# Weight-block sums from an accumulating DMA to VectorE, and the adaLN sums spread anew

## The chip, the cores and the metric

One core of one Trainium2 chip. The metric is the device time in microseconds of one execution; the time of a kernel is the median over its runs. The engines are named as in the profile: PE is TensorE (PEld its weight loads), DVE is VectorE, ACT is ScalarE, POOL is GpSimd, and SP is SyncE, which here issues nearly all DMAs.

## The reference

A two-layer trunk over 512 tokens of width 1024, in float32. Each layer is a token mixer and then a SwiGLU FFN, each between two RMSNorms, with shift, scale and gate from a conditioning vector `c` (adaLN):

```python
def ada_modulation(c, w, b):
    m = jax.nn.silu(c) @ w + b
    shift, scale, gate = jnp.split(m, 3, axis=-1)
...
for i in range(DEPTH):
    shift, scale, gate = ada_modulation(c, mix_ada_w[i], mix_ada_b[i])
    h = rms_norm(x, mix_pre_g[i]) * (1.0 + scale) + shift
    y = stick_breaking_mixer(...) if i % 2 == 0 else token_mixing_mixer(...)
    x = x + gate * rms_norm(y, mix_post_g[i])
    shift, scale, gate = ada_modulation(c, ffn_ada_w[i], ffn_ada_b[i])
    h = rms_norm(x, ffn_pre_g[i]) * (1.0 + scale) + shift
    y = (silu(h @ w_gate) * (h @ w_up)) @ w_down        # D_FF = 2816
    x = x + gate * rms_norm(y, ffn_post_g[i])
```

Layer 0 mixes with stick-breaking attention (16 heads), layer 1 with a gMLP (`u, v = split(gelu(h @ w_in))`, a layer norm and a position mixing of `v`, then `(u * v) @ w_out`).

## The kernel before

**Precision.** Every float32 product is made of three: `split` writes a high part (ACT copies into float32r) and a low part (DVE subtracts), and `mm3` issues high by high, high by low and low by high. So each 512 KB slab of weights costs one 128x1024 ACT copy (line 94) and one 128x1024 DVE subtraction (line 95) before PE can use it.

**Weights.** `stream` lists all slabs in the order of use. `wget` emits the splits some slabs ahead and `wload` the loads. Raw slabs live in `wraw` (2 buffers), split ones in `wpool` and `wpool2` (6 pairs in all).

**Stages in order.** Attention and its projection; a boundary (RMSNorms, adaLN, transposes of the new `h`); gate/up of FFN 0; its down projection; a boundary; the gMLP; a boundary; gate/up of FFN 1; its down projection. In each gate/up stage the first three of the 22 column groups are multiplied plainly (`unit`), the other 19 with a seven-product (Strassen-Winograd) scheme over two halves of tokens, of the inner dimension, and of gate against up (`seven`).

**A block of seven.** For each of the 19 blocks of a stage `block_loads` and `blocks` make the four sums of weight blocks that the scheme needs. `x` holds B11 and B22 and `y` holds B21 (`rawx`, `rawy`). `f13` holds T1 and T3: SP reads `wx` a second time into it, and a DMA on the POOL queue then adds the rest of `wy` with `accum_op=ALU.add` (line 152; in `wy` the block B12 lies twice for this). `f24` (T2, T4) is summed on DVE in two halves (lines 165 and 166). All are split. `seven` runs the products into three PSUM banks; between them ACT copies (lines 945, 949, 951) and DVE adds or subtracts (947, 953, 955), and PE goes on into the same banks. The last product (T4) can start when the subtraction of line 955 has read its bank; line 963 multiplies silu(gate) by up and ends the block.

**adaLN sums.** `ada_stt` (line 269) adds one 128x1024 slab of adaLN weights, scaled by a column of silu(c), to an accumulator on DVE: 8 sums for each of shift (B), scale (A) and gate (G) of a sub-layer. A `Bg` is a generator over such parts: first all sums, then for each part a reduction over partitions in two halves (split, two matmuls with ones into a bank `adaps`, an evacuation). `step(n)` advances it by n yields. The raw slabs `rawada` share the pool `raw2` (2 buffers) with `rawy`. Attention carries G0, A0 and B0. In the first gate/up stage `bg0` carries G1 and A1; in the first down stage `bg` carries B1 and G2 at two steps for each k until the cut `mid`, then `bg2` (A2, B2) at two steps for each k, with its rest in the gMLP; the second gate/up stage carries G3.

**The cut.** In the first down stage the sums over k of tile 0 lie in the two banks that `adaps` needs too. `mid` is the k at which they are copied out (`yp`), so that the reductions can run; it follows from the number of parts:

```python
mid = min(nk - J, -(-8 * len(bg.parts) // steps) + 1) if steps else None
```

With 2 parts and 2 steps `mid` is 9, with 3 parts it is 13; `nk - J` is 18.

**Order.** The order of each engine's instructions is made at compile time by a list scheduler from the program's order and the buffers; on the chip every engine and every DMA queue takes its instructions in that order. General slots (`slot`, pool `s4`) are 28 buffers of 4 KB per partition that hold nearly all activations.

Of the kernel before, what the change touches and what calls it, by code (L numbers as in the profile page):

```python
# [13 lines left out]
P = 128  # L14
# [12 lines left out]
def trunk(ctx: ExitStack, tc: tile.TileContext, A: dict, out: bass.AP):  # L27
# [110 lines left out]
    def block_loads(idx):  # L138

        fp = fwork["pool"]
        x = wraw.tile([P, KD, P], F32, tag="raw", name=nm("rawx"))
        y = fwork["raw"].tile([P, 4, P], F32, tag="raw2", name=nm("rawy"))
        f13 = fp.tile([P, KD, P], F32, tag="f13", name=nm("f13"))
        wx, wy = A["wx"][idx], A["wy"][idx]
        load(x[:], wx)
        load(f13[:], wx)  # L150
        load(y[:], wy[:, 0:4, :])
        nc.gpsimd.dma_start(out=f13[:], in_=wy[:, 4:12, :], accum_op=ALU.add)  # L152
        return x, y, f13

    def blocks(xr, yr, f13):

        fp = fwork["pool"]
        x = wtile(KD, P)
        split(x[0][:], x[1][:], xr[:])
        b21 = [fp.tile([P, 4, P], F32R, tag=f"b21{i}", name=nm("b21")) for i in range(2)]  # L160
        split(b21[0][:], b21[1][:], yr[:])
        t13 = wtile(KD, P)
        split(t13[0][:], t13[1][:], f13[:])
        f24 = fp.tile([P, KD, P], F32, tag="f24", bufs=1, name=nm("f24"))
        dve.tensor_tensor(f24[:, 0:4, :], f13[:, 0:4, :], xr[:, 4:8, :], ALU.add)
        dve.tensor_tensor(f24[:, 4:8, :], f24[:, 0:4, :], yr[:], ALU.add)
        t24 = wtile(KD, P)
        split(t24[0][:], t24[1][:], f24[:])

        def half(t, i):  # L170
            return lambda k: (t[0][:, 4 * i + k, :], t[1][:, 4 * i + k, :])

        return {
            "B11": half(x, 0), "B22": half(x, 1), "B21": half(b21, 0),
            "T1": half(t13, 0), "T3": half(t13, 1), "T2": half(t24, 0), "T4": half(t24, 1),
        }
# [98 lines left out]
    class Bg:  # L275
# [2 lines left out]

        def __init__(self, *parts):

            self.parts = [
                (n, int(s), int(s) + (n != "G"), {"G": 2, "A": 1, "B": 0}[n]) for n, s in parts
            ]
            self.gen = self.run()

        def run(self):
            for name, at, s, part in self.parts:
                acc = slot(F32, name, 1, D)[:, 0, :]  # L290
                ada[name, at] = acc
                nc.gpsimd.memset(acc, 0.0)
                load(acc[0:1, :], A["adab"][s, part])
                for k in range(KD):
                    raw = fwork["raw"].tile([P, D], F32, tag="raw2", name=nm("rawada"))
                    load(raw[:], A["ada"][s, part, k])
                    ada_stt(acc, raw[:], k)
                    yield
            for name, at, s, part in self.parts:
                acc = ada[name, at]  # L300
                if part:
                    row = A["pre_g"] if part == 1 else A["post_g"]
                    g = slot(F32, "g", 1, D)[:, 0, :]
                    load(g, row[s : s + 1, :].to_broadcast([P, D]))
                for b in range(2):
                    c = slice(b * 512, (b + 1) * 512)
                    h = adas.tile([P, 512], F32R, tag="acch", name=nm("acch"))
                    l = adas.tile([P, 512], F32R, tag="accl", name=nm("accl"))
                    split(h[:], l[:], acc[:, c])
                    yield  # L310
                    yield
                    ps = bank("adaps", "p")
                    mm(ps[:], ones_r, h[:], True, False, last_tp[0])
                    mm(ps[:], ones_r, l[:], False, True)
                    if part == 0:
                        act.activation(acc[:, c], ps[:], AF.Copy)
                    elif part == 1:
                        dve.scalar_tensor_tensor(acc[:, c], ps[:], 1.0, g[:, c], ALU.add, ALU.mult)
                    else:
                        dve.tensor_tensor(acc[:, c], ps[:], g[:, c], ALU.mult)  # L320
# [110 lines left out]
    def out_proj(s, nk, get_act, wkey, J, bg, hT, nxt=(), pre=None, S=None, steps=0, bg2=None):  # L431

        last = 0 if steps else 3
        mid = min(nk - J, -(-8 * len(bg.parts) // steps) + 1) if steps else None
        yp = None
        y = [[None, None] for _ in range(NT)]  # L440

        def step(k, tt, a, w, halves=(0, 1)):
            for hf in halves:
                if k == 0 or k == mid and tt == last:
                    y[tt][hf] = bank("y", "p" if tt == last else "b")
                mm3(
                    y[tt][hf][:],
                    a[0][:, tt * P : (tt + 1) * P], a[1][:, tt * P : (tt + 1) * P],
                    w[0][:, 0, hf * 512 : (hf + 1) * 512],
                    w[1][:, 0, hf * 512 : (hf + 1) * 512],  # L450
                    k == 0 or k == mid and tt == last, k == nk - 1 or k + 1 == mid and tt == last,
                )

        npre = 0
        if pre is not None:
            npre = len(pre["w"])
            for tt in pre["y"]:
                y[tt] = pre["y"][tt]
        for k in range(nk - J):
            a = get_act(k)  # L460
            w = pre["w"][k] if k < npre else wget(wkey(k))
            for tt in range(NT):
                if k >= npre or tt not in pre["y"]:
                    step(k, tt, a, w)
            bg.step(steps)
            if bg2 is not None and mid is not None and k >= mid:
                bg2.step(2)
            if k + 1 == mid:
                yp = slot(F32, "yp")
                for hf in range(2):  # L470
                    act.activation(yp[:, hf, :], y[last][hf][:], AF.Copy)
                bg.step(99)
        bg.step(99)
        tail = [
            (k, get_act(k), wget(wkey(k), J + 1 if k == nk - J else 0))
            for k in range(nk - J, nk)
        ]
        sqrt_table()
        xs = {tt: x_load(tt) for tt in range(2)}
        xin = xs.get  # L480
        for tt in range(NT):
            for hf in range(2):
                for k, a, w in tail:
                    step(k, tt, a, w, (hf,))
            if tt == last and yp is not None:
                for hf in range(2):
                    dve.tensor_tensor(yp[:, hf, :], y[tt][hf][:], yp[:, hf, :], ALU.add)
                y[tt] = [yp[:, hf, :] for hf in range(2)]
            if tt < 2:
                boundary(s, tt, y[tt], xin, hT, S, "p" if last == 0 else "b")  # L490
                xs[tt + 2] = x_load(tt + 2)
        evacs, late = [], []
        for n, tt in enumerate((2, 3)):
            if nxt:
                evacs.append(nxt[n]())
            late.append(boundary(s, tt, y[tt], xin, hT, S, "p" if tt == 3 else "b"))
        if nxt:
            evacs.append(nxt[2]())
            with tc.issue_after(last_sqrt[0].ins):
                for f in evacs:  # L500
                    f()
        if hT is not None:
            for f in late:
                f()
# [382 lines left out]
    class Ffn:  # L887
# [81 lines left out]
        def run(self, bg0, bg, bg2, steps, nhT, nxt, nS=None):  # L969
            for f in range(NH):  # L970
                self.unit(f, 256, 256)()
            for f in range(NH, KF):
                self.seven(f)()
                bg0.step(1 + (f % 3 == 0))
            bg0.step(99)
            out_proj(
                self.s, KF, lambda k: act_split(self.act[k // 2][:, k % 2, :]),
                lambda k: ("wdown", self.li, k), 4, bg, nhT, nxt, None, nS, steps, bg2,
            )
# [21 lines left out]
        return evac  # L1001

    uw = {}
    STEPS = 1

    def u_first(hT, ms):
        ev = []
# [5 lines left out]
    def gmlp(bg, hT, nhT, nS, nxt):  # L1013
# [114 lines left out]
    )  # L1128
    bg2 = Bg("A2", "B2")
    f0.run(  # L1130
        Bg("G1", "A1"), Bg("B1", "G2"), bg2, 2, hT2,
        [lambda a=a: u_first(hT2, range(a, min(a + 2, NU))) for a in range(0, NU, 2)],
    )
    gmlp(bg2, hT2, hT3, S3, f1.first())
    f1.run(Bg("G3"), bg2, None, 0, None, ())


def _layout(i):
# [7 lines left out]
    def blocks(a, b):  # L1146

        return (
            np.concatenate([a[:, :, :4], b[:, :, 4:]], 2),
            np.concatenate([a[:, :, 4:], b[:, :, :4], b[:, :, :4]], 2),  # L1150
        )

    def slabs(w):
# [77 lines left out]
```

## Time and profile before

| | us |
|---|---|
| median of 3 runs | 1222.86 (1219.6 to 1223.47) |
| the profiled execution | 1221.21 |
| its span, first to last instruction | 1219.5 |
| PE busy | 1176.3 |
| DVE busy | 846.6 |
| ACT busy | 621.3 |
| POOL busy | 51.4 |

The HBM moved 194.44 MB in and 8.39 MB out. The mean granted clock of PE was 0.998. In the profile a matmul's duration is longer than its share of PE, since matmuls overlap: those of 256 columns last 0.28 us and start 0.117 us apart, those of 512 columns last 0.395 us and start 0.232 us apart. So a block's length is read from the distance between starts, and what PE loses from its idle time before an instruction.

### The profile page before, as it was taken

The numbers are of one execution on the slowest core, as the hardware profiler recorded it, in microseconds if no ns is written. First come the engines' busy times: TensorE is split into PE (matmuls) and PEld (weight loads), VectorE is DVE, ScalarE is ACT, GpSimd is POOL, SyncE is SP. The second block draws the span as 40 slices with busy tenths as digits, with TensorE's granted clock in tenths as the row PEclk, the third lists the DMA queues.
The fourth block names the chain that finished last, engine by engine and source line by source line (L and its number), as shares of the span: only waits on it lengthen the run. The fifth ranks groups of instructions, "written<-read, shape, count | busy, mean of one in ns | idle before, by whom it ended". The sixth has DMA issues, their size and how long they took to land.

```text
span 1219.5 us, 18827 instructions
## 1 busy us (share of the span) xinstructions
PE 1176.3 (96%) x7408; PEld 1031.6 (85%) x7408; DVE 846.6 (69%) x1183; ACT 621.3 (51%) x1071; POOL 51.4 (4%) x68
## 2 busy tenths in 40 slices
PE   7898999999999999999999999999999999999997
PEld 4777778787899889998888898898998999998886
DVE  5878887766797787777787764567977777774223
ACT  6455767785564444556252453535644555573212
POOL 0100000000000010001000000000000001000000
PEclk9999999999999999999999999999999999999999
DMA  8666341121648868776888453314477777635311
GB/s 332 231 203 203 114 139 53 50 72 54 187 135 240 231 199 250 216 193 187 276 277 294 156 173 106 102 70 138 134 206 234 214 182 182 156 106 176 100 52 69
DMA packets 59580, 204.05 MB, mean 167 GB/s; under 512 B 6874, under 2 KB 7002, under 8 KB 59492
## 3 DMA queue, kind: packets, MB, share of 16 engines
q1 hardware_dynamic: 52292, 176.64, 43.2%
q0 software_dynamic: 7200, 26.22, 11.2%
q8 instruction: 58, 0.95, 0.3%
q14 instruction: 30, 0.25, 0.1%
HBM read 194.44 MB, written 8.39 MB: 166 GB/s over the span
## 4 chain that ended last, share of the span: by engine, by line
PE 66%; DVE 14%; DMA 11%; issue 4%; ACT 4%; DVEq 0%; SPq 0%; ACTq 0%
PE y L71 24%; PE r L71 19%; DMA rawada<-in_ada 7%; PE v L71 5%; PE pqk L71 4%; DVE wl L95 4%; PE u L71 3%; PE av L71 2%; PE z3h L71 2%; PE z0h L71 2%; DMA raw<-in_wgu 1%; PE gu L71 1%; ACT wh L94 1%; PE tp L79 1%; PE z2h L71 1%
## 5 line engine op out<-in xcount | busy, mean ns | idle before, releaser
L71 PE MATMUL y<-wh,as 128*128 128x512 f32 x832 | 263.5, 395 | 0.3 <-ACT gu L960 0.3
L94 ACT ACTIVATE wh<-raw 128x1024 fp32r<-128x1024 f32 x112 | 118.4, 1059 | 205.4 <-PE y L71 111.5
L95 DVE TENSOR_TENSOR wl<-raw,wh 128x1024 fp32r<-128x1024 f32 x112 | 136.6, 1221 | 123.4 <-ACT wh L94 123.3
L71 PEld LDWEIGHTS y<-wh,as 128*128 128x128 f32 x832 | 156.2, 188 | 37.0 <-ACT gu L960 0.7
L71 PE MATMUL r<-Sh,wh 128*128 128x256 f32 x608 | 171.7, 282 | 7.1 <-ACT e L951 4.1
L71 PE MATMUL r<-Sh,wl 128*128 128x256 f32 x608 | 170.2, 280 | 0.0
L71 PE MATMUL r<-Sl,wh 128*128 128x256 f32 x608 | 170.0, 280 | 0.0
L71 PE MATMUL y<-wl,as 128*128 128x512 f32 x416 | 164.3, 395 | 0.0
L94 ACT ACTIVATE wh<-f 128x1024 fp32r<-128x1024 f32 x76 | 80.7, 1061 | 92.0 <-PE r L71 82.6
L71 PEld LDWEIGHTS r<-Sh,wh 128*128 128x128 f32 x608 | 114.6, 189 | 10.2 <-ACT e L951 6.0
L71 PEld LDWEIGHTS r<-Sl,wh 128*128 128x128 f32 x608 | 114.5, 188 | 0.0
L71 PEld LDWEIGHTS r<-Sh,wl 128*128 128x128 f32 x608 | 114.4, 188 | 0.0
L95 DVE TENSOR_TENSOR wl<-f,wh 128x1024 fp32r<-128x1024 f32 x76 | 92.7, 1220 | 29.1 <-ACT wh L94 29.1
L71 PE MATMUL r<-hTh,wh 128*128 128x256 f32 x304 | 88.9, 294 | 8.3 <-DVE gu L955 8.0
L71 PEld LDWEIGHTS y<-wl,as 128*128 128x128 f32 x416 | 78.2, 188 | 18.1
L71 PE MATMUL r<-hTl,wh 128*128 128x256 f32 x304 | 84.9, 280 | 0.0
L71 PE MATMUL r<-hTh,wl 128*128 128x256 f32 x304 | 80.5, 281 | 0.0
L71 PEld LDWEIGHTS r<-hTh,wh 128*128 128x128 f32 x304 | 57.2, 188 | 15.1 <-DVE gu L955 12.3
L269 DVE SCALAR_TENSOR_TENSOR G<-rawada,sc,G 128x1024 f32<-128x1024 f32 x32 | 41.1, 1283 | 41.3 <-DMA rawada<-in_ada 39.2
L71 PE MATMUL r<-hTh,b 128*128 128x256 f32 x304 | 61.7, 286 | 0.0
L152 POOL DMA_DIRECT2D f<-in_wy x38 | 33.2, 881 | 645.6 <-ACT wh L94 262.6
L71 PEld LDWEIGHTS r<-hTl,wh 128*128 128x128 f32 x304 | 57.4, 189 | 0.2
(245 smaller groups left out, 2669.3 us busy)
## 6 DMA issues: line engine op xcount, KB each, us to landing
rawada<-in_ada SPq DMA_DIRECT2D x80, 512.0 KB, 4.3
raw<-in_wdown SPq DMA_DIRECT2D x44, 512.0 KB, 4.2
f<-in_wx SPq DMA_DIRECT2D x38, 512.0 KB, 4.9
f<-in_wy POOLq DMA_DIRECT2D x38, 512.0 KB, 5.9
rawx<-in_wx SPq DMA_DIRECT2D x38, 512.0 KB, 5.3
rawy<-in_wy SPq DMA_DIRECT2D x38, 256.0 KB, 2.9
raw<-in_wqk SPq DMA_DIRECT2D x16, 512.0 KB, 4.5
ada<-in_ada0p SPq DMA_DIRECT2D x12, 512.0 KB, 5.6
```

Source lines behind the costliest of these rows:

```text
L71: b = nc.tensor.matmul(o, l, r, start=start, stop=stop, skip_group_check=True)
L79: last_tp[0] = nc.tensor.transpose(o, i, ident)
L94: act.activation(hi, src, AF.Copy)
L95: dve.tensor_tensor(lo, src, hi.bitcast(F32), ALU.subtract)
L152: nc.gpsimd.dma_start(out=f13[:], in_=wy[:, 4:12, :], accum_op=ALU.add)
L269: dve.scalar_tensor_tensor(acc, w, sc[:, kk : kk + 1], acc, ALU.mult, ALU.add)
```

## The change

`f13` is no longer loaded and accumulated by DMA. `rawy` is read whole (512 KB, B12 in it once), and one DVE instruction sums `rawx` with B12 read twice. The sum stands behind the split of B21 in `blocks`.

The `Bg` gets a switch `slots`: with it the raw adaLN slabs come from the general slots, and the generator yields between a slab's load and its sum, so that one slab is asked for a step ahead. G1 and G3, in the gate/up stages, use it. `bg0` steps once after those blocks whose number isn't divisible by 3 (before: once, and twice after those divisible by 3). A1 moves to the first down stage, whose `bg` has three parts (A1, B1, G2); `bg2` steps once for each k behind the cut, and twice for each k of the gMLP's `v` (`STEPS`).

```diff
-        y = fwork["raw"].tile([P, 4, P], F32, tag="raw2", name=nm("rawy"))
-        f13 = fp.tile([P, KD, P], F32, tag="f13", name=nm("f13"))
-        wx, wy = A["wx"][idx], A["wy"][idx]
-        load(x[:], wx)
-        load(f13[:], wx)
-        load(y[:], wy[:, 0:4, :])
-        nc.gpsimd.dma_start(out=f13[:], in_=wy[:, 4:12, :], accum_op=ALU.add)
-        return x, y, f13
+        y = fwork["raw"].tile([P, KD, P], F32, tag="raw2", name=nm("rawy"))
+        load(x[:], A["wx"][idx])
+        load(y[:], A["wy"][idx])
+        return x, y
...
-        split(b21[0][:], b21[1][:], yr[:])
+        split(b21[0][:], b21[1][:], yr[:, 0:4, :])
+        f13 = fp.tile([P, KD, P], F32, tag="f13", name=nm("f13"))
+        dve.tensor_tensor(
+            f13[:].rearrange("p (a k) f -> p a (k f)", a=2),
+            xr[:].rearrange("p (a k) f -> p a (k f)", a=2),
+            yr[:, 4:8, :].rearrange("p (a k) f -> p a (k f)", a=1).to_broadcast([P, 2, 512]),
+            ALU.add,
+        )
...
-                    raw = fwork["raw"].tile([P, D], F32, tag="raw2", name=nm("rawada"))
-                    load(raw[:], A["ada"][s, part, k])
-                    ada_stt(acc, raw[:], k)
-                    yield
+                    if self.slots:
+                        raw = slot(F32, "rawada", 1, D)[:, 0, :]
+                    else:
+                        raw = fwork["raw"].tile([P, D], F32, tag="raw2", name=nm("rawada"))[:]
+                    load(raw, A["ada"][s, part, k])
+                    if self.slots:
+                        yield
+                    ada_stt(acc, raw, k)
+                    if not self.slots:
+                        yield
...
             if bg2 is not None and mid is not None and k >= mid:
-                bg2.step(2)
+                bg2.step(1)
...
                 self.seven(f)()
-                bg0.step(1 + (f % 3 == 0))
+                if f % 3:
+                    bg0.step(1)
...
-    STEPS = 1
+    STEPS = 2
...
-        Bg("G1", "A1"), Bg("B1", "G2"), bg2, 2, hT2,
+        Bg("G1", slots=True), Bg("A1", "B1", "G2"), bg2, 2, hT2,
...
-    f1.run(Bg("G3"), bg2, None, 0, None, ())
+    f1.run(Bg("G3", slots=True), bg2, None, 0, None, ())
...
-            np.concatenate([a[:, :, 4:], b[:, :, :4], b[:, :, :4]], 2),
+            np.concatenate([a[:, :, 4:], b[:, :, :4]], 2),
```

More of the change, by code (lines that the diff above doesn't have):

```diff
@@ L138, in block_loads, with blocks @@
     def block_loads(idx):
-        fp = fwork["pool"]
         x = wraw.tile([P, KD, P], F32, tag="raw", name=nm("rawx"))
-        y = fwork["raw"].tile([P, 4, P], F32, tag="raw2", name=nm("rawy"))
-        f13 = fp.tile([P, KD, P], F32, tag="f13", name=nm("f13"))
-        wx, wy = A["wx"][idx], A["wy"][idx]
-        load(x[:], wx)
-        load(f13[:], wx)
-        load(y[:], wy[:, 0:4, :])
-        nc.gpsimd.dma_start(out=f13[:], in_=wy[:, 4:12, :], accum_op=ALU.add)
-        return x, y, f13
-    def blocks(xr, yr, f13):
+        y = fwork["raw"].tile([P, KD, P], F32, tag="raw2", name=nm("rawy"))
+        load(x[:], A["wx"][idx])
+        load(y[:], A["wy"][idx])
+        return x, y
+    def blocks(xr, yr):
         fp = fwork["pool"]
@@ L165, in blocks @@
         dve.tensor_tensor(f24[:, 0:4, :], f13[:, 0:4, :], xr[:, 4:8, :], ALU.add)
-        dve.tensor_tensor(f24[:, 4:8, :], f24[:, 0:4, :], yr[:], ALU.add)
+        dve.tensor_tensor(f24[:, 4:8, :], f24[:, 0:4, :], yr[:, 0:4, :], ALU.add)
         t24 = wtile(KD, P)
@@ L275, in trunk, with __init__ @@
     class Bg:
-        def __init__(self, *parts):
+        def __init__(self, *parts, slots=False):
+            self.slots = slots
             self.parts = [
```

## The prediction

> **What bounds the kernel now.** The page comes first. It gives the span and the share of each engine; the profiled execution took 1221.21 us around a span of 1219.5 us, 1.65 us below the median of the three runs (1222.86 us).
>
> ```profile
> span 1219.5 us, 18827 instructions
> PE 1176.3 (96%) x7408; PEld 1031.6 (85%) x7408; DVE 846.6 (69%) x1183; ACT 621.3 (51%) x1071; POOL 51.4 (4%) x68
> ```
>
> PE is busy 96%, and the change takes nothing from PE, so only PE's idle time can be won. The second view cuts the span into its stages. Columns: length, then busy time of PE, PEld, DVE, ACT and POOL, granted clock, DMA share, GB/s. The rows are first gate/up, first down, its boundary, gMLP, second gate/up.
>
> ```profile
> 346.00:577.00 231.00, 220.23 (x1791) 214.34 (x1790) 178.28 (x245) 118.78 (x200) 19.85 (x23) 0.99 0.73 207
> 577.00:692.00 115.00, 115.00 (x503) 92.85 (x502) 87.09 (x92) 39.57 (x58) 2.03 (x3) 1.00 0.80 265
> 692.00:717.00 25.00, 24.49 (x166) 22.13 (x166) 22.54 (x32) 16.67 (x36) 2.14 (x4) 1.00 0.42 139
> 717.00:870.00 153.00, 152.29 (x917) 134.03 (x916) 92.61 (x121) 70.94 (x112) 3.08 (x5) 1.00 0.37 120
> 870.00:1091.00 221.00, 216.31 (x1783) 211.69 (x1782) 164.47 (x230) 116.58 (x196) 14.77 (x17) 1.00 0.64 175
> ```
>
> The reader is to see that PE loses 231.00 - 220.23 = 10.8 us in the first gate/up stage and 4.7 us in the second, and nothing in the first down stage. The two gate/up stages are also where DVE is fullest (178.28 of 231.00) and where the change works. The same view, cut finer at the ends of blocks (one block of seven products ends with the DVE multiply of line 963), shows which blocks lose the time:
>
> ```profile
> 383.71:438.25 54.54, 50.75 (x413) 48.90 (x412) 42.63 (x58) 26.73 (x46) 5.28 (x6) 1.00 0.79 228
> 438.25:505.76 67.51, 62.88 (x506) 61.32 (x506) 51.84 (x70) 32.36 (x54) 5.23 (x6) 0.97 0.78 222
> 505.76:565.87 60.11, 60.11 (x498) 59.04 (x497) 43.58 (x63) 31.60 (x54) 5.51 (x7) 1.00 0.73 193
> 907.31:952.43 45.12, 42.33 (x347) 40.97 (x345) 35.14 (x47) 21.48 (x37) 3.46 (x4) 1.00 0.79 228
> 961.54:1073.40 111.86, 111.86 (x930) 110.07 (x929) 80.64 (x115) 59.28 (x99) 8.68 (x10) 1.00 0.66 175
> ```
>
> The first row is 5 blocks beside the sums of G1, the second 6 beside A1, the fourth 4 beside G3. The third (6 blocks) and the fifth (11) have no sums. Blocks without sums take (60.11 + 111.86) / 17 = 10.1 us and PE never idles. Blocks with sums take 10.9, 11.25 and 11.3 us. Against 10.1 each, the stretches lose 3.9 (G1), 6.8 (A1) and 4.6 us (G3), 15.3 in all. In the A1 stretch the granted clock is 0.97, so up to 3% of 67.51, 2.0 us, of its loss is clock rather than waiting.
>
> The waits say how. PE waits for the gate/up evacuations, and DVE stands before the sums; of the last three rows the first two are from the first gate/up stage, the third from the second:
>
> ```profile
> PE r L71 <- DVE gu L955: 8.0, 8, 1.8
> PE r L71 <- ACT e L951: 4.1, 8, 1.0
> DVE G L269 <- DMA rawada<-in_ada: 13.6, 7, 2.8
> DVE A L269 <- DMA rawada<-in_ada: 12.3, 6, 3.5
> DVE G L269 <- DMA rawada<-in_ada: 12.8, 6, 3.3
> ```
>
> DVE works in order: while it stands 2 to 3 us for a raw adaLN slab, the subtraction of line 955 stands behind it, and the product T4 on PE behind that. One such block in the timeline:
>
> ```profile
> 410.51 0.33 SPq L88 DMA_DIRECT2D rawada<-in_ada  x1
> 412.34 0.39 PE L71 MATMUL r<-hTh,wh 128*128 128x256 f32 x1 [1.50 <-DVE gu L955]
> 416.18 1.29 DVE L269 SCALAR_TENSOR_TENSOR G<-rawada,sc,G 128x1024 f32<-128x1024 f32 x1 [2.77 <-DMA rawada<-in_ada]
> ```
>
> **The change part by part.** The prices:
>
> ```profile
> L95 DVE TENSOR_TENSOR wl<-rawx,wh 128x1024 fp32r<-128x1024 f32 x38 | 46.4, 1220 | 8.7 <-ACT wh L94 8.6
> L269 DVE SCALAR_TENSOR_TENSOR G<-rawada,sc,G 128x1024 f32<-128x1024 f32 x32 | 41.1, 1283 | 41.3 <-DMA rawada<-in_ada 39.2
> L152 POOL DMA_DIRECT2D f<-in_wy x38 | 33.2, 881 | 645.6 <-ACT wh L94 262.6
> 1036.77 0.42 DVE L953 TENSOR_TENSOR gu<-r,e 128x256 f32<-128x256 f32 x1 [0.76 <-PE r L71]
> 1037.68 1.22 DVE L95 TENSOR_TENSOR wl<-rawx,wh 128x1024 fp32r<-128x1024 f32 x1 [0.49 <-ACT wh L94]
> 1038.83 0.41 DVE L955 TENSOR_TENSOR gu<-e,r 128x256 f32<-128x256 f32 x1
> 1041.99 1.22 DVE L95 TENSOR_TENSOR wl<-f,wh 128x1024 fp32r<-128x1024 f32 x1 [1.62 <-ACT wh L94]
> ```
>
> *f13 on DVE.* Each of the 38 blocks gains one two-input sum of 128x1024 in SBUF. The trace has no such sum with a repeated operand; the nearest row is the weight subtraction, 1.22 us (its successor starts 1.15 us later: 1037.68 to 1038.83). So 19 x 1.22 = 23.2 us in each gate/up stage. In a block without sums DVE waits 0.76 + 0.49 + 1.62 = 2.87 of 10.1 us, all for ACT or PE: the sum fits and leaves 2.87 - 1.15 = 1.7 us. I cost it at nothing where that cover holds. If the cover is gone (a wait in front of it, next paragraph), each block is late by what goes over 1.7 us.
>
> *The loads.* SP loses the second read of wx (38 x 512 KB), the POOL queue loses 38 accumulating transfers (33.2 us of POOL, which nobody but f13 waited for), and rawy grows from 256 to 512 KB. Per block 1792 KB become 1024 KB; at 10.1 us that is 78 GB/s less. SP issues one transfer less per block, 0.33 us. New is that DVE itself now waits for both rawx and rawy in front of f13. Lower bound 0: both are asked for about a block ahead. Upper bound: the sums' own kind of wait, 13.6 / 8 = 1.7 us per block, which would just use up the 1.7 us left. I take 0.05 us of loss per block over the 22 blocks without sums, 1.1 us, near the lower bound, since rawx and rawy each have two buffers to themselves once the sums leave them. The ends are 0 and, by the sums' loss of 15.3 / 15 = 1.0 us per block, 22 us.
>
> *G1 and G3 through general slots.* Eight sums per stage stay (twelve steps over the f with f % 3 not 0). Each slab has a slot of its own, is asked for one step ahead, and no longer queues behind rawy's release. How far the wait falls is bounded by landing times:
>
> ```profile
> DMA to landing us min/median/max: 3.5/4.8/6.1
> raw<-in_wout SPq DMA_DIRECT2D x8, 512.0 KB, 3.5
> ```
>
> A slab lands in 4.8 us in the first gate/up stage at 207 GB/s, and a slab of wout, in the quieter gMLP stage (120 GB/s), in 3.5. So 1.3 of the 1.7 us can go by lighter traffic alone, and all by the earlier request. The Trainium skill agrees in direction: "DMA: Bandwidth & Descriptors", section "Latency and other measured facts", gives HBM access as 0.2 us on average and 2 us at high load. By that page alone, as an estimate, the whole 1.7 us would be load, and the two stretches would lose nothing.
> A sum's block then has 2.87 - 1.15 - 1.20 = 0.5 us of DVE to spare, less what is left of the wait. Before, it had 2.87 - 1.20 - 1.7 = 0 and lost 0.8 to 1.1. I take 0.5 us for each of 16 sums, halfway, since the spare time is little better while the waits are shorter: 8.0 us where G1 and G3 lost 8.5. Ends 0 and 16 x 1.1 = 17.6.
>
> *A1 leaves the gate/up stage.* Its 6.8 us of loss goes. Its 8 sums (10.3 us of DVE) run in the first down stage.
>
> *The first down stage.* 24 sums stand before the middle cut instead of 16, and the cut moves from k = 9 to k = 13. From the tile and chain views:
>
> ```profile
> L269 DVE SCALAR_TENSOR_TENSOR B<-rawada,sc,B x16: 1274/1284/1286, 572.8 to 673.8; 128x1024 f32<-128x1024 f32 x16
> L269 DVE SCALAR_TENSOR_TENSOR G<-rawada,sc,G x8: 1283/1284/1285, 599.2 to 619.6; 128x1024 f32<-128x1024 f32 x8
> L269 DVE SCALAR_TENSOR_TENSOR A<-rawada,sc,A x8: 1274/1284/1285, 629.9 to 650.8; 128x1024 f32<-128x1024 f32 x8
> 577.63 49.21 PE y L71 x212
> ACT wh L94 <- DMA raw<-in_wdown: 20.2, 5, 7.2
> ```
>
> 16 sums took 572.8 to 620.8, 3.0 us each. PE's y products run at 49.21 / 212 = 0.232 us, 24 for each k, 5.57 us. Before, PE came to the cut at 577.6 + 9 x 5.57 = 627.8, 7 us after the last sum; now it comes at 650.0 and 24 sums end at 644.8, 5 us ahead. Six halves are reduced there instead of four, between y products. I take 0; ends 0 and 5. ACT already waits 20.2 us for wdown there without PE noticing; the pace of wdown is unchanged, and the stage has 29 sums instead of 32.
>
> *A2 and B2 late.* From 650 on, 5 sums lie in the down stage and 11 behind it. On raw2's two buffers they ran at (675.1 - 629.9) / 16 = 2.8 us; at that pace they would reach 695, into the boundary, where DVE is busy 22.54 of 25.00 us. In gMLP DVE has 60 us free, and 12 steps of two hold the 19 steps that are left. I take +1 us; ends 0 and 11 x 1.28 = 14.
>
> The sum: -6.8 (A1) - 0.5 (G1, G3) + 1.1 (f13's cover) + 1.0 (boundary) = -5.2 us. 1221.21 - 5.2 = 1216.0 in the profiled execution's terms, 1217.7 in the median's. I say 1217.5.
>
> **The rivals.** (a) *Slower: f13 makes DVE stand for its loads in every block.* Its place is DVE's queue ahead of lines 953 and 955, because the next block's sums are issued ahead of this block's evacuations. For it: the sums stood 2.77 us in just that place. Against it: rawx's subtraction stood 8.7 us for ACT in 38 blocks and for no transfer. It decides from a wait of 1.7 us on. At 1.0 us lost in half of the 22 free blocks, and 1.1 in each of the 16 others, it gives 11 + 17.6 + 1.0 = 29.6 instead of 15.3: 1222.86 + 14 = 1237; with a third of that, 1228. The Trainium skill speaks for this rival: "Perfetto Trace Analysis", section "Optimizing Scalar/DVE Operations", advises breaking an instruction up where a DVE that isn't saturated causes bubbles on other engines, and the change adds one of the longest kind. The trace agrees as far as the 1.22 us subtraction in front of line 955 above goes, though PE does not idle there.
> (b) *No change: what A1 gives back is eaten.* G1 and G3 keep their full 1.0 us per sum (16 us), and f13 costs 1.1: 17.1 + 1 against 15.3 is +2.8; with 0.8 us per sum, -0.4. That is 1222 to 1225. For it: DVE's spare time beside a sum barely changes (0 to 0.5 us).
> (c) *Faster than forecast: all blocks run at 10.1 us.* Then 15.3 us go and 1 comes back: 1208.6. For it: the 17 blocks without sums averaged that, and a block with a sum asks 10.1 - 2.87 + 1.15 + 1.20 = 9.6 us of DVE.
> (d) *Slower by the boundary alone.* The 11 late sums stand in DVE's queue among the boundary's chain: +7 or more where six of them do. It decides when more than four land between 692 and 717: about 1224 to 1228 with the gains left.
>
> **How the numbers follow.** Within 0.3% (3.7 us) a measurement of this kernel can't tell a difference. Forecast 0.36 (1212 to 1219), (c) 0.16, (b) 0.22, (a) 0.19, (d) 0.07. Faster is forecast and (c), 0.52; same is (b), 0.22; slower is (a) and (d), 0.26. The range runs from (c) to the milder half of (a): 1208 to 1232.
>
> **What would show it.** Right: the gate/up windows at 10.1 to 10.6 us a block throughout, the sums' DMA waits on DVE below 0.8 us each there, PE waits on line 955 below 5 us, the first down stage still without PE idle, the sums of A2 and B2 ending in gMLP. Wrong: a DVE wait of f13 on rawx or rawy (a), blocks without sums above 10.3 us (a), PE idle near the reductions of the cut or between 692 and 717 (d), G1 and G3 blocks still at 11 us (b).

## The result and the profile after

The changed kernel takes 1205.17 us in the median (1203.4 to 1208.33) against 1223.16 for the kernel before: a ratio of 0.9861, 95% interval 0.9833 to 0.989. The forecast was 1217.5 us. The time fell by more than three times the 5.2 us of the sum, below the low end of the range, and closest to rival (c).

The first lines of the page of the changed kernel:

```profile
span 1201.6 us, 18615 instructions
PE 1170.4 (97%) x7408; PEld 1029.0 (86%) x7408; DVE 885.1 (74%) x1221; ACT 623.4 (52%) x1071; POOL 18.2 (2%) x30
```

DVE works 38.5 us longer than before and the span is 17.9 us shorter. To see where, the span is cut at PE's own work: the front up to the first seven-product matmul (`r`), the stage of seven-product matmuls, the first down stage with its boundary, and so on, each from the first or last start of that kind of matmul in the timeline. Microseconds of the profiled executions:

| stage | before | after |
|---|---|---|
| front, to the first `r` | 367.7 | 367.5 |
| first gate/up, its 19 blocks of seven | 209.7 | 192.9 |
| first down stage and boundary | 125.4 | 129.7 |
| gMLP: `u` first part | 30.8 | 31.1 |
| gMLP: `v` | 46.4 | 48.1 |
| gMLP: rest, boundary, plain gate/up | 111.1 | 111.2 |
| second gate/up, its 19 blocks of seven | 200.6 | 193.5 |
| second down stage | 121.3 | 121.3 |

The two gate/up stages gave 16.8 + 7.1 = 23.9 us, and the first down stage and `v` took 4.3 + 1.7 = 6.0 back. Up to 2.0 us of the 16.8 is the granted clock and not waiting: it was 0.97 in the prediction's A1 window of before (67.51 us), and is 1.00 over the whole stage after. The same cut in the view by windows, the columns as in the prediction; before:

```profile
367.69:577.36 209.67, 198.90 (x1610) 193.01 (x1609) 157.80 (x213) 107.38 (x182) 19.32 (x22) 0.99 0.77 217
891.04:1091.60 200.56, 195.87 (x1609) 191.25 (x1608) 146.87 (x203) 106.54 (x181) 13.89 (x16) 1.00 0.67 185
```

and after, with the first down stage in the middle:

```profile
367.51:560.36 192.85, 192.85 (x1606) 190.03 (x1604) 165.31 (x223) 107.97 (x182) 2.87 (x3) 1.00 0.42 132
560.36:690.06 129.70, 126.87 (x555) 101.84 (x554) 97.98 (x109) 46.04 (x74) 2.55 (x4) 1.00 0.74 245
880.46:1073.98 193.52, 193.52 (x1608) 190.53 (x1606) 163.57 (x220) 108.46 (x182) 0.00 (x0) 1.00 0.39 124
```

In both gate/up stages PE is now busy from end to end (192.85 of 192.85, 193.52 of 193.52), while DVE does more there than before (165.31 against 157.80, 163.57 against 146.87). No wait of DVE for an adaLN slab is left in either stage. The timeline of SP's queue shows the requests for the first two slabs of G1, right behind one for `rawx` (start, length, engine, line):

```profile
387.07 0.33 SPq L88 DMA_DIRECT2D rawx<-in_wx  x1
387.45 0.43 SPq L88 DMA_DIRECT2D rawada<-in_ada  x1
388.26 0.33 SPq L88 DMA_DIRECT2D rawada<-in_ada  x1
```

and the timeline of DVE the two sums themselves:

```profile
397.33 1.28 DVE L270 SCALAR_TENSOR_TENSOR G<-rawada,sc,G 128x1024 f32<-128x1024 f32 x1
398.53 1.22 DVE L95 TENSOR_TENSOR wl<-f,wh 128x1024 fp32r<-128x1024 f32 x1
399.67 1.28 DVE L270 SCALAR_TENSOR_TENSOR G<-rawada,sc,G 128x1024 f32<-128x1024 f32 x1
```

The sums stand 9.9 and 11.4 us behind their requests, and neither row has a bracket, that is, no idle time in front of it. In the block that the prediction showed the distance was 416.18 - 410.51 = 5.7 us, with 2.77 us of waiting. Pairing the k-th request with the k-th sum over a whole stage gives 3.5 to 9.7 us before, with waits of 0.9 to 3.5 us at 12 of the 16 sums of G1 and A1, and 7.1 to 11.5 us after, with none. A wait is part of its distance: where a sum waits, the distance is just the time in which its slab landed. With the wait taken off, DVE came to its sums in the median 3.0 and 2.9 us behind the requests before (first and second stage), and 8.0 us after. By the landing of every slab in the traces (the view by tile places only some of them), the slabs took 3.5 to 7.2 us before, with a median of 5.1 in each stage, and 4.8 to 7.0 us after, with a median of 6.0.

### The profile page after: what moved, and what is told of

Read it like the earlier page. It is cut to its first block, busy times and chain, and to the rows that moved or that the text cites. A ratio compares the mean times of both kernels' runs of the same rounds, so it can differ in the third digit from the quotient of the medians.

```text
span 1201.6 us, 18615 instructions
## 1 busy us (share of the span) xinstructions
PE 1170.4 (97%) x7408; PEld 1029.0 (86%) x7408; DVE 885.1 (74%) x1221; ACT 623.4 (52%) x1071; POOL 18.2 (2%) x30
## 4 chain that ended last, share of the span: by engine, by line
PE 74%; DVE 10%; DMA 10%; ACT 3%; issue 3%; SPq 0%; DVEq 0%; ACTq 0%
PE r L71 31%; PE y L71 19%; DMA rawada<-in_ada 6%; PE pqk L71 4%; PE gu L71 4%; PE v L71 3%; PE av L71 2%; PE u L71 2%; DVE wl L95 2%; PE z3h L71 2%; PE z0h L71 2%; DVE B L270 1%; DVE A L270 1%; ACT wh L94 1%; PE tp L79 1%
## 5 line engine op out<-in xcount | busy, mean ns | idle before, releaser
L94 ACT ACTIVATE wh<-rawx 128x1024 fp32r<-128x1024 f32 x38 | 40.4, 1062 | 35.3 <-PE r L71 30.9
L71 PEld LDWEIGHTS r<-hTh,wl 128*128 128x128 f32 x304 | 55.2, 188 | 0.0
```

Of the source, the lines that this page charges most:

```text
L71: b = nc.tensor.matmul(o, l, r, start=start, stop=stop, skip_group_check=True)
L94: act.activation(hi, src, AF.Copy)
```

## The experiments

In the table *distance* is from a slab's request to its sum, *waits* is the time that DVE stood for slabs in front of adaLN sums; both in the stage of blocks of seven, first and second, for G1 (with A1, where it is there) and G3. Stage lengths are cut as above. Every kernel has line numbers of its own: the subtraction of line 955 is line 961 with f13 by DMA again, 960 in "slots, no step", and 963 in the changed kernel, "no general slots" and "step, no slots"; the sums of `ada_stt` are at lines 268 to 271.

| kernel | ratio to before (95%) | first gate/up | second gate/up | first down | `v` | waits | distance |
|---|---|---|---|---|---|---|---|
| before | 1 | 209.7 | 200.6 | 125.4 | 46.4 | 25.9, 12.8 | 3.5 to 9.7, 3.6 to 6.3 |
| changed | 0.9861 (0.9833 to 0.989) | 192.9 | 193.5 | 129.7 | 48.1 | 0, 0 | 7.1 to 11.4, 7.1 to 11.5 |
| f13 by DMA again | 0.9883 (0.9849 to 0.9916) | 196.6 | 196.8 | 130.1 | 47.4 | 4.7, 4.5 | 5.3 to 9.9, 5.8 to 9.9 |
| only f13 on DVE | 0.987 (0.984 to 0.99) | 197.8 | 197.5 | 126.9 | 46.4 | 4.0, 5.1 | 3.5 to 9.9, 3.5 to 6.0 |
| no general slots | 0.9885 (0.9843 to 0.9928) | 196.1 | 197.5 | 129.0 | 47.7 | 3.0, 2.4 | 3.5 to 19.8, 3.5 to 22.9 |
| A1 back in gate/up | 0.9815 (0.9784 to 0.9845) | 196.3 | 193.5 | 126.0 | 46.4 | 1.2, 0 | 5.3 to 17.2, 7.1 to 11.3 |
| slots, no step | 0.9855 (0.98 to 0.9909) | 194.6 | 195.3 | 130.4 | 48.1 | 0, 0 | 7.1 to 10.3, 7.1 to 10.3 |
| step, no slots | 0.9924 (0.9889 to 0.9959) | 197.9 | 198.8 | 127.9 | 47.7 | 3.7, 1.9 | 3.5 to 19.8, 3.5 to 22.9 |
| f13 twice | 0.9857 (0.9805 to 0.9908) | 194.0 | 192.3 | 130.3 | 47.7 | 0.2, 0.3 | |
| all sums through slots | 0.9808 (0.977 to 0.9847) | 193.0 | 193.5 | 127.1 | 46.4 | 0, 0 | |
| extra transfers | 0.9915 (0.9886 to 0.9944) | 198.7 | 200.0 | 128.0 | 47.8 | 0, 0 | 7.1 to 10.6, 7.1 to 10.6 |
| all slots, A1 in gate/up | 0.981 (0.9785 to 0.9835) | 195.3 | 193.5 | 126.2 | 46.4 | 0.9, 0 | |
| all slots, old tail | 0.98 (0.9776 to 0.9825) | 192.5 | 193.5 | 127.0 | 46.4 | 0, 0 | |
| f13 by DMA, sums held back | 0.9836 (0.9796 to 0.9875) | 194.0 | 193.6 | 128.1 | 46.9 | 0, 0 | 13.0 to 32.5, 13.1 to 32.7 |

The front varies by up to 5.5 us between these profiled executions (365.8 to 371.3); the granted clock of its first 66 us was 0.97 with f13 by DMA again and with A1 back, against 1.00 in the changed kernel. So the stages are compared, and not the spans.

### The parts of the change, one at a time

**f13 by DMA again**, the new spread kept:

```diff
-        load(y[:], A["wy"][idx])
-        return x, y
+        load(f13[:], wx)
+        load(y[:], wy[:, 0:4, :])
+        nc.gpsimd.dma_start(out=f13[:], in_=wy[:, 4:12, :], accum_op=ALU.add)
+        return x, y, f13
```

> The changed kernel with f13 loaded and accumulated by DMA again, as before; the new spread of the adaLN sums stays (G1, G3 through general slots a step early, A1 in the first down stage). The seven-product stages took 209.7 and 200.7 us before and 192.9 and 193.7 us after. Theory W (the loss was DVE standing in order for adaLN slabs; asking for them early removes it): both stages within 2 us of after, 193 to 195, the kernel at 1203 to 1208 us. Rival T (the loss was traffic, and the change won by moving 30 MB less): both stages stay above 199, the kernel at 1213 or more. Rival A (only A1's place matters): first stage about 200, second at 200.

Measured: 196.6 and 196.8 us, 1212.65 us in the median. Neither theory holds whole: two thirds of the gain stay (410.3 before, 393.4 here, 386.4 with the change, for both stages), and a third goes. What is left of the waits in its first gate/up stage:

```profile
DVE G L268 <- DMA rawada<-in_ada: 4.7, 4, 1.5
PE r L71 <- DVE gu L961: 3.2, 3, 1.2
```

DVE still stands for slabs, less often, and PE behind the same subtraction as before (line 961 here).

**Only f13 on DVE**: the sums' spread and buffers as before.

```diff
 (the kernel before, with)
+        load(x[:], A["wx"][idx])
+        load(y[:], A["wy"][idx])
+        return x, y
...
+        dve.tensor_tensor(f13[:]..., xr[:]..., yr[:, 4:8, :]....to_broadcast([P, 2, 512]), ALU.add)
```

> The kernel before with f13 summed on DVE and rawy loaded whole; the adaLN sums are spread and buffered as before. Theory W: the sums' slabs still queue behind rawy in the two buffers of raw2, so the DMA waits of G1, A1 and G3 on DVE stay above 1 us each, and DVE has 1.15 us less to spare: stages at 205 to 220 and 200 to 208, the kernel at 1218 to 1235 us. Rival T: with the traffic gone the waits fall below 0.5 us each, stages at 195 to 200, the kernel at 1207 to 1212.

Measured: 197.8 and 197.5, 1211.47 us. The expectation of theory W is missed, and rival T's stages and time came: the waits fall from 25.9 to 4.0 us in the first stage, although all 16 sums of G1 and A1 are in it and use raw2. What is left there:

```profile
DVE A L271 <- DMA rawada<-in_ada: 3.3, 5, 0.9
DVE G L271 <- DMA rawada<-in_ada: 0.7, 2, 0.4
```

In the second stage the waits fall from 12.8 to 5.1 us, and 0.5 to 1.2 us are left in front of six sums. The distances hardly changed, since a sum that waits starts when its slab lands. Two other times moved, each by about 1 us. The slabs landed in 4.2 and 4.3 us (medians of the two stages) against 5.1 before, so with f13's transfers gone the landings did grow shorter. And DVE, its waits taken off, came to its sums 4.0 and 3.9 us behind the requests, against 3.0 and 2.9. So this run does not tell traffic from distance.

**No general slots** for G1 and G3 (their slabs in raw2, summed at once):

```diff
-        Bg("G1", slots=True), ...
+        Bg("G1"), ...
-    f1.run(Bg("G3", slots=True), ...
+    f1.run(Bg("G3"), ...
```

> The changed kernel, but G1 and G3 take their slabs from raw2 and sum at once, as before; A1 stays in the down stage, f13 on DVE. Theory W: DMA waits of G1 and G3 come back, 1 to 1.7 us each, and with them 4 to 8 us in each of the two stages: 197 to 201, the kernel at 1212 to 1221. Rivals T and A: the stages stay within 2 us of after, the kernel at 1203 to 1209.

Measured: 196.1 and 197.5, 1211.59 us: the first stage just below theory W's range, the second within it, and the time just below its range. The waits come back, but only 3.0 and 2.4 us of them; beside them f13 stands for rawy, which shares raw2 with the slabs:

```profile
DVE G L270 <- DMA rawada<-in_ada: 3.0, 5, 1.0
PE r L71 <- DVE gu L963: 2.8, 4, 1.1
DVE f L157 <- DMA rawy<-in_wy: 2.6, 6, 0.8
```

This is the wait of rival (a), 2.6 and 4.1 us in the two stages. It is there when slabs take raw2's buffers; in the changed kernel f13 waits 0.5 us in all 38 blocks, and for `rawx`.

**A1 back in the first gate/up stage**, beside G1, through slots and at the old pace of steps:

```diff
-                if f % 3:
-                    bg0.step(1)
+                bg0.step(1 + (f % 3 == 0) if len(bg0.parts) > 1 else int(f % 3 > 0))
...
-        Bg("G1", slots=True), Bg("A1", "B1", "G2"), bg2, 2, hT2,
+        Bg("G1", "A1", slots=True), Bg("B1", "G2"), bg2, 2, hT2,
```

> The changed kernel with A1 back in the first gate/up stage beside G1, both through general slots a step early, at the old pace of 26 steps; the cut of the down stage is at k = 9 again. Theory W: the first stage stays within 3 us of after (193 to 196), since no slab is waited for; DVE is then asked for 10.1 - 2.87 + 1.15 + 1.20 = 9.6 us in most blocks; the down stage loses less at its cut, so the kernel is at 1201 to 1206. Rival A (DVE's time is what counts): the first stage goes back to 198 or more, the kernel at 1208 to 1214.

Measured: 196.3 and 193.5, 1204.45 us. The stage lies just above theory W's range, and the time within it. A1's eight sums cost 3.4 us there, half of the 6.8 us that they cost without slots (up to 2.0 of which was clock), and the down stage and `v` give back 3.7 and 1.7. So A1's new place is not what gained the time.

### Which part of the early request counts

**Slots without the step** between load and sum:

```diff
                     load(raw, A["ada"][s, part, k])
-                    if self.slots:
-                        yield
                     ada_stt(acc, raw, k)
-                    if not self.slots:
-                        yield
+                    yield
```

> The changed kernel, but in G1 and G3 the generator yields behind the sum again: general slots, no step between a slab's load and its sum. If the step between them is what ends the waits: G1 and G3 stand for their slabs on DVE for 2 to 5 us in each gate/up stage, and the seven-product stages take 196 to 198 us each instead of 192.9 and 193.5. If the separate buffers do it: no waits, stages within 1 us of after.

**The step without slots**:

```diff
-                    if self.slots:
+                    if False:
                         raw = slot(F32, "rawada", 1, D)[:, 0, :]
```

> The changed kernel, but the slabs of G1 and G3 lie in raw2 beside rawy again, with the step between load and sum kept. If the separate buffers matter: a slab held a step longer in one of raw2's two buffers makes rawy late, f13 stands on DVE for rawy, stages at 197 or more. If the step alone does it: within 1 us of 192.9 and 193.5.

The first gave 194.6 and 195.3 us, no wait for a slab, and distances of 7.1 to 10.3 us. What it lost against the changed kernel goes with rival (a)'s wait, 1.5 us in each stage, and PE idle for 1.4 us behind line 960; in the first stage:

```profile
DVE f L157 <- DMA rawy<-in_wy: 1.5, 3, 1.0
```

The second gave 197.9 and 198.8 us and 1213.58 us, as its first expectation said. Its first gate/up stage, in DVE's and PE's waits and in those of SP's queue:

```profile
PE r L71 <- DVE gu L963: 3.9, 4, 1.3
DVE G L270 <- DMA rawada<-in_ada: 3.7, 5, 1.2
DVE f L157 <- DMA rawy<-in_wy: 3.2, 5, 1.1
SPq L88 <- DVE G L270: 9.7, 7, 1.9
```

The last row is SP, which asks in order, standing seven times for a sum of G to let go of the buffer that the next `rawy` needs. Buffers of its own give a slab its early request; the step in the program gives little beside them (1.7 and 1.8 us), and nothing without them (196.1 and 197.5 us with neither), because slabs and `rawy` then wait for each other's buffers.

### Is DVE's spare time as small as counted

```diff
+        dve.tensor_tensor(f13[:]..., xr[:]..., yr[:, 4:8, :]..., ALU.add)
         dve.tensor_tensor(f13[:]..., xr[:]..., yr[:, 4:8, :]..., ALU.add)
```

> The changed kernel with every f13 sum issued twice (the second writes the same values again): 1.15 us more of DVE in each of 38 blocks. By the prediction's count a block without a sum then asks 9.5 of 10.1 us of DVE, one with a sum 10.7. If that count holds: +0.6 us for each of 8 sums, stages at 197 to 199 and 198 to 200. If DVE's spare time is larger than counted, within 1 us of 192.9 and 193.5. If f13's place ahead of the evacuations costs PE anything, all 38 blocks grow, stages above 200.

```profile
368.90:562.90 194.00, 192.08 (x1606) 189.98 (x1605) 186.12 (x243) 111.36 (x186) 2.88 (x3) 1.00 0.41 133
888.00:1080.00 192.00, 191.69 (x1585) 189.04 (x1585) 183.44 (x241) 112.18 (x186) 0.00 (x0) 1.00 0.40 127
```

DVE is busy 186.12 of 194.00 us, 96%, and the stages are 194.0 and 192.3 us long, against 192.9 and 193.5: 1.1 us more and 1.2 us less, 386.3 against 386.4 together. The middle expectation holds to 0.2 us: 38 more sums of 1.22 us cost nothing. Of PE's 1.9 idle us in the first stage 1.7 lie ahead of the blocks, where it waits for ACT. A full DVE does not hold PE up here; a DVE that stands does.

### Bytes or distance

**Extra transfers**: the bytes per block of before, read into spare general slots behind `rawx` (`bx` is its load).

```diff
+        for m in (8, 4):
+            z = slot(F32, "spare", KD, P)
+            order(nc.sync.dma_start(out=z[:, :m, :], in_=A["wx"][idx][:, :m, :]), bx)
```

> The changed kernel with two more plain transfers per block, 512 and 256 KB of wx, asked for behind rawx on SP into general slots and read by nobody: the bytes per block are those of before (1792 KB), without the accumulating DMA and without its queue. If bytes alone make the slabs late: landing of the slabs in the gate/up stages rises from 4 to 6 us or more, DVE stands 3 to 6 us for slabs in each, the stages take 195.5 to 198 as with f13 accumulated by DMA (196.6, 196.8). If it was the accumulating DMA: no waits, within 1 us of 192.9 and 193.5.

The run took 1213.89 us, and its stages 198.7 and 200.0. Both expectations are missed in part, so the stage has to be opened. Sixteen blocks in a row of the first stage, from the end of the first block, in the view by windows; in the kernel before:

```profile
383.71:557.01 173.30, 164.88 (x1339) 160.55 (x1338) 133.92 (x182) 87.08 (x147) 14.86 (x17) 0.99 0.78 218
```

in the changed one:

```profile
381.17:542.24 161.07, 161.07 (x1344) 158.90 (x1344) 139.96 (x188) 87.30 (x145) 0.00 (x0) 1.00 0.42 135
```

and in this one:

```profile
388.80:549.46 160.66, 160.66 (x1342) 158.65 (x1341) 140.46 (x188) 87.48 (x145) 0.00 (x0) 1.00 0.60 209
```

The view of the slabs' tile, in the same stage of this kernel:

```profile
DMA to landing us min/median/max: 3.4/6.0/8.6
```

At 209 GB/s, as many as before (218), and with slabs landing in 6.0 us (the median of the three landings that this view could place), the blocks take 160.66 us, as long as in the changed kernel, and no sum waits. What this kernel loses lies ahead of the blocks. PE waits there for the token sums of the scheme (`Sh`, `Sl`), whose tiles are general slots too, and in the first stage the granted clock is low as well: 0.83 over 19.90 us, where the changed kernel takes 13.66 us at 1.00. The window, and PE's waits of both stages:

```profile
368.90:388.80 19.90, 17.23 (x119) 16.71 (x118) 15.27 (x24) 10.39 (x17) 0.00 (x0) 0.83 0.36 120
PE r L71 <- ACT Sh L94: 5.4, 2, 3.7
PE r L71 <- DVE Sl L95: 1.7, 2, 0.9
```

That the spare slabs held those slots is likely and was not tried. Within the blocks, as many bytes as before cost nothing where sums stand 7.1 us and more behind their requests.

**f13 by DMA, sums held back**: the first experiment once more, with each sum ordered behind the last multiply of the block in front of it.

```diff
-                    ada_stt(acc, raw, k)
+                    b = ada_stt(acc, raw, k)
+                    if self.slots:
+                        order(b, last_mul[0])
```

> The kernel of the run with f13 accumulated by DMA and the new spread, with one more order: each of G1's and G3's sums is issued on DVE behind the last multiply of the block just finished, so never earlier than a block after its slab's request. In that run slabs landed in 6.4 us at about 200 GB/s, sums stood 5.3 to 9.9 us behind their requests, DVE waited 4.7 and 4.5 us for them, and the stages took 196.6 and 196.8. If what counts is only the distance between a slab's request and its sum: distances above 7 us, waits below 1 us, stages at 193 to 194.5 as with f13 on DVE, and the kernel within 0.3% of the changed one. If f13's accumulation costs PE something by itself: waits gone, stages still above 195.5.

Measured: 194.0 and 193.6 us, 1203.36 us, 0.9836 of before (0.9796 to 0.9875). Its two gate/up stages, with 38 accumulating DMAs on POOL and 210 and 192 GB/s:

```profile
367.34:561.30 193.96, 193.32 (x1605) 190.13 (x1604) 146.57 (x201) 107.61 (x182) 19.53 (x22) 1.00 0.74 210
878.34:1071.99 193.65, 193.65 (x1607) 190.43 (x1606) 147.04 (x203) 107.98 (x183) 14.89 (x17) 1.00 0.68 192
```

Slabs land in 6.4 and 6.2 us here, the sums stand 13 us and more behind their requests, no sum waits, and PE is idle for 0.64 us in the first stage and not at all in the second. So the distance accounts for all but 1.2 us of the two gate/up stages (387.6 against 386.4), and moving f13 to DVE gains no more than that by itself once the sums are late enough. In the first experiment sums stood as little as 5.3 us behind their requests, and slabs landed in 5.3 to 7.5 us. That f13 on DVE fills the gaps in which a sum was issued early is read from the distances (5.3 to 9.9 against 7.1 to 11.5 us), not tried alone.

### What the first down stage lost

**All sums through slots**:

```diff
-        Bg("G1", slots=True), Bg("A1", "B1", "G2"), bg2, 2, hT2,
+        Bg("G1", slots=True), Bg("A1", "B1", "G2", slots=True), bg2, 2, hT2,
...
-    bg2 = Bg("A2", "B2")
+    bg2 = Bg("A2", "B2", slots=True)
```

> The changed kernel with all later sums (A1, B1, G2, A2, B2) through general slots a step early as well. After the change the first down stage with its boundary took 129.7 us (125.4 before) and v 48.1 (46.4); DVE stood 19 us for slabs there, and PE 2.5 us for the reductions at the cut. If those waits are late requests: they fall below 6 us, the stage goes to 125 to 127 and v to 46.5, the kernel to 1199 to 1202. If the stage is bound by its transfers (24 slabs and 13 of wdown in 72 us, 270 GB/s): the waits move to wdown, the stage stays at 129 or more.

In the changed kernel, by the waits in its first down stage, PE waited at the cut for the reductions, and ACT, in front of them, for wdown:

```profile
ACT wh L94 <- DMA raw<-in_wdown: 33.2, 9, 10.5
DVE G L270 <- DMA rawada<-in_ada: 8.9, 8, 2.4
DVE B L270 <- DMA rawada<-in_ada: 7.6, 7, 2.0
PE adaps L71 <- ACT acch L94: 2.5, 1, 2.5
```

With slots for all sums the waits for slabs and PE's wait are gone, and ACT's wait for wdown is halved. The window of the stage:

```profile
560.44:687.51 127.07, 127.07 (x557) 102.14 (x555) 95.79 (x108) 49.51 (x80) 3.52 (x5) 1.00 0.64 228
```

and the waits in it:

```profile
ACT wh L94 <- DMA raw<-in_wdown: 15.0, 6, 4.1
```

The stage falls to 127.1 (just above the range expected), `v` to 46.4, the kernel to 1199.84 us. Late requests, not the bytes, made up 2.6 of the stage's 4.3 us and all of `v`'s 1.7.

**All slots, A1 in gate/up** (there at the old pace of steps), and **all slots, old tail** (two steps of `bg2` for each k, one in `v`), both against the kernel with all sums through slots:

```diff
-        Bg("G1", slots=True), Bg("A1", "B1", "G2", slots=True), bg2, 2, hT2,
+        Bg("G1", "A1", slots=True), Bg("B1", "G2", slots=True), bg2, 2, hT2,
```
```diff
-                bg2.step(1)
+                bg2.step(2)
...
-    STEPS = 2
+    STEPS = 1
```

> All adaLN sums after attention through general slots a step early, and A1 back in the first gate/up stage, so 16 sums instead of 24 before the cut. First gate/up stage as with A1 back alone (196.3), the down stage at 125 to 125.5 (127.1 with 24 sums through slots, 125.4 before), v 46.4. If A1's price in gate/up (3.4 us) is larger than what the down stage gives back (1.7 us), the kernel is 1 to 2 us slower than with A1 in the down stage (0.981 of before); otherwise equal or faster.

> All sums after attention through general slots a step early, A1 in the down stage, and A2, B2 at the old pace (two steps for each k behind the cut, one in v). If the down stage's last 1.7 us (127.1 against 125.4) come from sums that fall into the boundary or from the slower tail: 125.4 to 126, the kernel 1 us faster than 0.981 of before. If they come from six halves at the cut instead of four: unchanged at 127, the kernel at 0.980 to 0.982.

The first has 195.3 in gate/up and 126.2 in the down stage, at 0.981; the second 127.0, at 0.98. Their intervals overlap that of the kernel with all sums through slots, so none of the three is shown to be the fastest. The tail's pace is not where the last 1.7 us of the down stage are. A1's own reduction, four matmuls of 0.23 us on PE, moved there from gate/up with A1: 0.9 us of it, which is also the difference to the kernel with A1 in gate/up (127.1 to 126.2). The other 0.8 us is open.

## Why the prediction was wrong

**The mechanism** was right: DVE stood in order for late slabs, and PE behind line 955. It was confirmed by the runs without slots, with the sums held back, and with f13 twice. What failed are three terms of the sum: the one for G1 and G3, the loss of before, and the down stage.

**The term for G1 and G3 was mis-sized.** The prediction took 0.5 us of loss for each of 16 sums (8.0 us) because it counted DVE's spare time, 0.5 us a block, as what a sum's block lacks. Measured is 0: with a distance of 7.1 us or more, where slabs land in 4.8 to 7.0, no sum waits, and the run with f13 twice shows that a DVE 96% full costs PE nothing. The 8.5 us of G1 and G3 go whole. A sum's loss hung on standing still, not on how much DVE had to do, and halfway between two bounds was the wrong value: the step from one to the other is a threshold, the landing time.

**The loss of before was counted too low.** The windows ran over 15 blocks beside sums, 15.3 us. They left out the start of each stage, from its first `r` to the end of the first block: 16.0 and 16.3 us before, 13.7 in both stages after, 4.9 us together. Three of the eight sums of G1 and three of G3 stand in that start, with 3.4 us of waits for slabs each time. The end of the first stage, from the 17th block's end (557.01 and 542.24), took 20.3 us before and 18.1 after, another 2.2; the 18th block lay in a window taken as free of loss, the 19th in none, and why they lost is open. 15.3 + 4.9 + 2.2 = 22.4 of the 23.9 us gained. Rival (c), all blocks at 10.1 us, was what happened in these stages. That its time was only 3.4 us too high is partly luck: it missed 8.6 us of gain there and 5.0 us of cost in the down stage and `v`.

**A1**'s loss of 6.8 us, up to 2.0 of it clock, went, but its move was not needed to end half of it: with slots A1 costs 3.4 us in gate/up. **f13's cover** holds: 1.1 us was taken, none is seen. Its instruction measured what the nearest row had said:

```profile
L157 DVE TENSOR_TENSOR f<-rawx,rawy 128x1024 f32<-128x1024 f32 x38 | 46.2, 1217 | 0.5 <-DMA rawx<-in_wx 0.5
```

1217 ns, and 0.5 us of waiting in all 38: rival (a) did not come. Buffers of its own for rawy were not enough for that: with slots and no step f13 stood 1.5 us for rawy in each stage, and with slabs in raw2 2.6 to 5.5 us. The Trainium skill's advice that was put beside this rival ("Perfetto Trace Analysis", section "Optimizing Scalar/DVE Operations", to break up instructions that cause bubbles elsewhere) found no bubble to remove here: two of them in a row did no harm.

**The loads' landing time did not fall** in the changed kernel, though the step rested on it. Slabs landed in 6.0 us (median of each gate/up stage) at 132 and 124 GB/s, against 5.1 us at 217 and 185 GB/s before. They are asked for 0.4 to 1.2 us behind rawx there, as the queue's rows of the first stage show (387.07, 387.45, 388.26); in the kernel with the step and no slots they mostly go out ahead of it, and landed in 3.6 us (median) at 129 and 121 GB/s. The Trainium skill's "DMA: Bandwidth & Descriptors", section "Latency and other measured facts", lets the fixed cost fall with a lighter load. The run with only f13 on DVE agrees in direction (4.2 and 4.3 us against 5.1); in the changed kernel, with its slabs right behind rawx, the landings grew, and the waits went all the same.

**The down stage** was taken at 0 and the boundary at +1; together with `v` they cost 6.0 us. The forecast that 24 sums end before PE reaches the cut came true (the last sum of G2 ends at 628.4, PE's first product of a reduction behind it runs at 632.0; the forecast was 5 us ahead). What failed was taking the six halves as hidden between y products: PE stood 2.5 us for the second of them, until 636.7, since ACT, in order, stood for wdown in front of its split (4.9 and 0.8 us at the two copies before it). Rival (d) is refuted in its place: no PE wait above 0.8 us lies in the boundary, and the late sums of B2 ran on to 737.7 in `v`.

## What to carry to other kernels

For an engine that works in order, find how long after a transfer's request the engine comes to its use, any wait taken off, and set that against the landing time; that decides whether all that stands behind it is late, far more than how busy the engine is. Background loads need buffers of their own: in a pool shared with foreground loads they are asked for only when the other lets go, whatever the program's order says. And when a loss is summed by windows, let the windows cover the whole stage, from the bound engine's first instruction to its last.

## What was not expected of the hardware

Plain 512 KB loads asked for 0.4 to 1.2 us behind another one landed in 4.8 to 7.0 us (the changed kernel, median 6.0, 132 and 124 GB/s), where the same loads, mostly asked for ahead of it, landed in 3.4 to 5.3 us (step, no slots, median 3.6, 129 and 121 GB/s). A request's neighbours in the queue went with a larger difference than the mean traffic, whose fall from 217 and 185 GB/s went with 0.7 to 0.8 us in the run with only f13 on DVE. No run changed the neighbours alone. And 38 accumulating DMAs of 512 KB, with thirty megabytes more from HBM and the POOL queue's work, cost PE no more than 1.2 us over both stages when no in-order wait hung on their neighbours.
